# The output projection of a gated convolution, with its block product done as seven products of halves

## The chip, the cores and the metric

One NeuronCore of one Trainium2 chip runs the whole kernel. The metric is the device time of one execution in microseconds (us); smaller is better. The engines are named as the profile names them: PE (TensorE: matmuls, with PEld for its weight loads), DVE (VectorE), ACT (ScalarE), POOL (GpSimd) and SP (SyncE, which here only issues DMA transfers).

## The reference

One layer of a diffusion trunk on 1024 tokens of width 1024, float32. `ada_terms` makes six rows from a conditioning vector. The change is in the line `(gate_b * conv) @ w_out` and the two after it:

```python
def short_conv_mixer(h, w_in, conv_w, w_out, on_grid):
    gate_b, gate_c, hv = jnp.split(h @ w_in, 3, axis=-1)
    u = gate_c * hv
    conv = conv3_grid(u, conv_w) if on_grid else conv3_seq(u, conv_w)
    return (gate_b * conv) @ w_out

def swiglu(h, w_in, w_out):
    gate, up = jnp.split(h @ w_in, 2, axis=-1)
    return (jax.nn.silu(gate) * up) @ w_out

# in reference(), the one layer there is:
sh1, sc1, g1, sh2, sc2, g2 = ada_terms(cond_lat, ada_w[i], ada_b[i])
hl = modulate(rmsnorm(x, norm1_g[i]), sh1, sc1)
yl = short_conv_mixer(hl, conv_w_in[j], conv_w[j], conv_w_out[j], True)
x = x + g1 * yl
x = x + g2 * swiglu(modulate(rmsnorm(x, norm2_g[i]), sh2, sc2), ffn_w_in[i], ffn_w_out[i])
return rmsnorm(x, final_g)
```

## The kernel before, in words

**Numbers.** Every float32 operand of a matmul is kept as two tiles, a high half (a cast on ACT) and a low half (raw minus high, on DVE; `split`, lines 82 to 84). A product of two operands is three matmuls: high by high, high by low, low by high (`TERMS`). A matmul here is 128 by 128 times 128 by 512.

**Seven products.** The projections `h @ w_in`, `h @ ffn_w_in` and the last one, `@ ffn_w_out`, cut both matrices into two by two quarters and form the block product with seven products of (sums of) quarters instead of eight; they are named P1 to P7. P1, P6, P7 and P4 add up in one PSUM bank (X), P2 goes to Y, P5 and P3 go to Z. The convolution's output projection `@ w_out` alone is the plain product.

**Stages on PE, in the order of time.** First the adaLN columns and the first projection products (lines 421, 472). Then the mixes (line 522): 60 steps of 12 matmuls, six pairs of output tiles by five products. Then the output projection (line 1108): `y_steps` for eight tiles of 128 tokens. For a tile, eight pieces of 128 channels by two halves of the columns by three terms are 48 matmuls, with the token tile stationary and 512 columns of `w_out` moving. After a tile, `residual` (lines 1114 to 1139) multiplies by the row g1, adds x, takes the mean square and the scaled rows `xr`; `h2_of` (lines 1075 to 1090) transposes them on PE and applies the second shift and scale while PE leaves PSUM. Then the FFN: `Gate` objects (line 1183 on), each with seven products (line 632), the first three of them interleaved (`two`, `three`), the others in `in_turn`. Last the products of `ffn_w_out` (line 1537).

**What sets the order.** Up to the end of the mixes the order on SP, DVE, ACT and PE is written out by hand (`in_order`): at step t, first the loads of `ahead[t][0]` go to SP, then the sums and splits of the step, then the units of `ahead[t][1]`, then the 12 matmuls and what reads their result. POOL is left to the planner. From the output projection on, before the change, the planner of the tile framework orders all engines by priority, with a few `issue_after`.

**Tiles.** SBUF tiles come from pools with a fixed number of slots: `t_s` 32 slots of 4 KB a partition, `t_wop` 8 (halves of operands), `t_wraw` 5 (raw weights), `t4` 3, `t2` 6. A tile that finds no free slot makes its first writer wait. PSUM has 8 banks.

**Side work.** `AdaRow` objects `rows[0]` to `rows[5]` build the rows g1 (0, 1) and shift and scale for the second norm (2 to 5, into the DRAM row `rows3`): loads, scaling on ACT, an accumulating DMA on POOL, sums on DVE, a split, two matmuls over the partitions (line 291), an ACT copy (line 297) and a POOL store (line 299). `columns2` (lines 1141 to 1148) reads `rows3` back, transposes it on PE and makes `shift2` and `scale2`, which `h2_of` needs. The mixed channels, v, go to the DRAM tensor `vd` and come back as token tiles (`v_tile`).

## Time and profile before

| | us |
|---|---|
| Time, median of 3 runs (lowest, highest) | 989.28 (988.66, 989.86) |
| Span of the profiled execution, first to last instruction | 987.3 |
| PE busy in it | 978.7 |
| DVE, ACT, POOL busy in it | 721.0, 488.7, 121.3 |
| Mixes, by the chain of waits | 92.1 to 257.2 |
| Output projection | 257.2 to 351.4 |
| First three gates of the FFN | 351.4 to 412 |

The page gives no time for the profiled execution but its span; the runs' median stands 2.0 us above it (989.28 - 987.3). A matmul is shown with its own duration, about 0.39 us, but matmuls overlap: PE's rate is read from the chain of waits, where a row gives the time that so many matmuls in a row took. "PE busy" near 100% says only that PE is never without a matmul.

### The profile page before, as it was taken

To read this page: it belongs to the slowest core of one execution; us is meant where nothing else is said; L and a number is where in the kernel's file an instruction comes from. 1 tells how busy PE (TensorE), PEld (TensorE's weight loads), DVE (VectorE), ACT (ScalarE), POOL (GpSimd) and SP (SyncE) were. 2 spreads that over 40 slices of the span, in tenths; PEclk is the share of its full clock that TensorE was granted. 3 is DMA by queue.
4 is the path that set the end of the run, shared out by engine and by line. 5 is a ranking of instruction groups with operands and counts; after the bars stand their busy time and mean duration, and the time that the engine had idled before them with its cause. 6 is when DMAs were issued, how large, how long until landed. Compare 5 with 4: busy or idle time off the path is not lost.

```text
span 987.3 us, 12316 instructions
## 1 busy us (share of the span) xinstructions
PE 978.7 (99%) x4416; PEld 807.3 (82%) x4416; DVE 721.0 (73%) x1014; ACT 488.7 (49%) x784; POOL 121.3 (12%) x201
## 2 busy tenths in 40 slices
PE   9999999999999999999999999999999999999997
PEld 6788888887888888888888888888888888888886
DVE  6968988888656799765865765665665755878898
ACT  6766776656445675333333333333334353534464
POOL 2031001121111100320130110110110110000300
PEclk9999999999999999999999999999999999999999
DMA  9999399997874232633642331431315954577534
GB/s 298 318 340 321 99 274 280 296 283 222 251 229 149 86 120 86 179 118 96 197 123 75 128 118 58 146 117 54 128 65 202 388 189 155 175 260 278 186 107 170
DMA packets 156733, 181.77 MB, mean 184 GB/s; under 512 B 8406, under 2 KB 113086, under 8 KB 156672
## 3 DMA queue, kind: packets, MB, share of 16 engines
q1 hardware_dynamic: 143088, 138.50, 44.0%
q0 software_dynamic: 12784, 40.17, 13.1%
q10 hardware_dynamic: 800, 2.32, 0.6%
q8 instruction: 34, 0.56, 0.2%
q14 instruction: 27, 0.22, 0.1%
HBM read 135.33 MB, written 38.03 MB: 176 GB/s over the span
## 4 chain that ended last, share of the span: by engine, by line
PE 97%; DVE 1%; DMA 1%; ACT 0%; issue 0%; SPq 0%; POOL 0%; DVEq 0%; ACTq 0%
PE X_f L632 24%; PE zP L1537 21%; PE m L522 17%; PE Z_f L632 12%; PE y L1108 9%; PE Y_f L632 6%; PE x L421 3%; PE x L472 3%; DVE ada_acc L180 1%; PE x1T L1081 1%; DMA x<-in_x_dram 1%; PE xT L348 1%; PE ada_ps L192 1%; PE zl L1537 0%; PE ada_ps L291 0%
## 5 line engine op out<-in xcount | busy, mean ns | idle before, releaser
L74 DVE TENSOR_TENSOR BP_f<-wr_f,BP_f 128x512 fp32r<-128x512 f32 x154 | 105.0, 687 | 63.4 <-ACT BP_f L83 61.3
L83 ACT CAST BP_f<-wr_f 128x512 fp32r<-128x512 f32 x154 | 94.8, 621 | 88.1 <-PE Z_f L632 62.8
L1537 PE MATMUL zP<-w3h_P,a3l_P 128*128 128x512 f32 (+1 forms) x308 | 118.6, 385 | 0.0
L1537 PE MATMUL zP<-w3l_P,a3h_P 128*128 128x512 f32 (+1 forms) x308 | 118.6, 385 | 0.0
L1537 PE MATMUL zP<-w3h_P,a3h_P 128*128 128x512 f32 (+1 forms) x308 | 117.2, 385 | 0.0
L1537 PEld LDWEIGHTS zP<-w3h_P,a3h_P 128*128 128x128 f32 x308 | 57.9, 188 | 11.7
L1537 PEld LDWEIGHTS zP<-w3l_P,a3h_P 128*128 128x128 f32 x308 | 57.9, 188 | 11.7
L1537 PEld LDWEIGHTS zP<-w3h_P,a3l_P 128*128 128x128 f32 x308 | 57.9, 188 | 11.4
L74 DVE TENSOR_TENSOR a3l_P<-a3l_P,a3h_P 128x1024 fp32r<-128x1024 f32 (+1 forms) x42 | 47.2, 1129 | 21.7 <-ACT a3h_P L1337 21.7
L632 PE MATMUL X_f<-AS3h,BP_f 128*128 128x512 f32 x176 | 57.7, 389 | 0.0
L632 PE MATMUL X_f<-A22h,BP_f 128*128 128x512 f32 x176 | 57.6, 389 | 0.0
L632 PE MATMUL Z_f<-AS4h,BP_f 128*128 128x512 f32 x176 | 57.6, 389 | 0.0
L632 PE MATMUL X_f<-AS2h,BP_f 128*128 128x512 f32 x176 | 57.6, 389 | 0.0
L632 PE MATMUL Y_f<-A12h,BP_f 128*128 128x512 f32 x176 | 57.5, 390 | 0.0
L632 PE MATMUL X_f<-A11h,BP_f 128*128 128x512 f32 x176 | 57.4, 389 | 0.0
L632 PE MATMUL Z_f<-AS1h,BP_f 128*128 128x512 f32 x176 | 57.4, 389 | 0.0
L1108 PE MATMUL y<-woh,vh_t 128*128 128x512 f32 x128 | 50.4, 394 | 0.0
L1108 PE MATMUL y<-woh,vl_t 128*128 128x512 f32 x128 | 49.9, 390 | 0.0
L1108 PE MATMUL y<-wol,vh_t 128*128 128x512 f32 x128 | 49.8, 389 | 0.0
L74 DVE TENSOR_TENSOR wr_f<-wr_f,wr_f 128x512 f32<-128x512 f32 x66 | 45.3, 688 | 1.6
L1337 ACT CAST a3h_P<-a3l_P 128x1024 fp32r<-128x1024 f32 (+1 forms) x42 | 40.7, 977 | 10.4 <-DMA a3l_P<-ad_S 6.9
L77 DVE TENSOR_TENSOR u_f<-Z_f,u_f 128x512 f32<-128x512 f32 x22 | 15.2, 690 | 37.9 <-ACT u_f L649 35.4
(349 smaller groups left out, 2371.4 us busy)
## 6 DMA issues: line engine op xcount, KB each, us to landing
wr_f<-in_ffn_w_in_dram SPq DMA_DIRECT2D x44, 512.0 KB, 3.7
ada_w<-in_ada_w_dram SPq DMA_DIRECT2D x60, 256.0 KB, 5.8
w_P<-in_ffn_w_out_dram SPq DMA_DIRECT2D x30, 512.0 KB, 5.7
a3l_P<-ad_S SPq DMA_DIRECT2D x20, 512.0 KB, 6.8
ad<-a POOLq DMA_DIRECT2D x33, 256.0 KB, 2.6
ada_w<-in_ada_w_dram SPq DMA_DIRECT2D x16, 512.0 KB, 5.4
a3l_P<-ad SPq DMA_DIRECT2D x15, 512.0 KB, 3.7
wr<-in_conv_w_in_dram SPq DMA_DIRECT2D x12, 512.0 KB, 8.0
```

The source lines that it names most:

```text
L74: return nc.vector.tensor_tensor(o, a, b, op=ALU.subtract)
L77: return nc.vector.tensor_tensor(o, a, b, op=ALU.add)
L83: nc.scalar.copy(hi, raw)
L180: nc.vector.scalar_tensor_tensor(acc, self.rows[r], by, acc, op0=ALU.mult, op1=ALU.add)
L192: nc.tensor.matmul(self.ps[j][:, j:j + 1], lhsT=part[:, j, :], rhs=by, start=j == 0 and r == (*self.direct, "sum")[0], stop=j == 1 and r = ...
L421: nc.tensor.matmul(xbank[pair], lhsT=w0[k][wi][:, place[pair], :], rhs=h_of(k, 0)[hi], start=(k == 0 and i == 0), stop=(k == KD - 1 and i ...
L472: nc.tensor.matmul(xbank[self.pair], lhsT=self.w[wi][:, k, :], rhs=h_of(half * KH + k, 0)[hi], start=(half == 0 and k == 0 and i == 0), st ...
L522: nc.tensor.matmul(self.ps[a], lhsT=self.w[pname][wi][:, k, a * P:(a + 1) * P], rhs=A[aname, k // 2][hi][:, k % 2, :], start=(q == 0 and k ...
L632: mm = nc.tensor.matmul(ps, lhsT=w[:, wi, 2 * kp + kk, :], rhs=A[aname, kp][hi][:, kk, :], start=(first and kp == 0 and kk == 0 and i == 0 ...
L1108: mm = nc.tensor.matmul(ys[t][n], lhsT=vt[t][vi][:, k, :], rhs=wo[k][wi][:, n * H:(n + 1) * H], start=(k == 0 and i == 0), stop=(k == KD - ...
L1337: nc.scalar.copy(hi, f(lo))
L1537: mm = nc.tensor.matmul((zs[t] if to is None else to)[:, cols], lhsT=a[ai][:, k % 2, t * P:(t + 1) * P], rhs=w[wi][:, k % 2, cols], start= ...
```

## The change

The output projection becomes seven products of halves too. The token tile j (of the first 512 tokens) and the tile j + 4 (of the last 512) are a pair; channels and columns are cut into halves. For each of seven products there are four steps, one for each pair, of 12 matmuls (two `kp`, two `n`, three terms), in the fixed order P1, P2, P5, P6, P7, P4, P3; they are the steps 60 to 87, and the first 17 steps of the FFN's first three gates follow as steps 88 to 104, in the same written order. Step 60 is called `Y0`, step 88 `F0`.

- g1 is multiplied into the quarters of `w_out` (`w_scale`, on DVE) instead of into the result. Sums of quarters of `w_out` are formed in place on DVE (`ws`, `w2`, `w4`, `n`), one sum of the token operand on DVE (`vs`), the others by accumulating DMAs on POOL (`v+`).
- Signs are put into the mixes (`mul_negated`) and into P6's weights.
- Half of v stays in SBUF; `vd` has four channel tiles, not eight.
- x is added by accumulating DMAs on POOL for the left half of the first tokens' columns and for all of the last tokens'; for the right half of the first tokens' it is loaded on SP into the tile to which P4's result is added. The scaling by 1/rms goes from ACT to DVE (`x`), `h2_of` becomes `h2_pair` (two tiles at once, in the middle of a product's matmuls, `mid`).
- The sums of `rows[4]` and `rows[5]` move from steps 49 to 58 to the steps 70 to 74, their matmuls to the steps 79 and 77; `load_rows3` goes from POOL to SP at step 80; `columns2` is at step 83.
- The load of g1 goes to step 50. The loads of the first three gates go to the steps 69, 72 and 74, their sums and splits one by one (`gs`, `gh`, `gl`) to the steps 74 to 100.
- In `in_turn`, loads of ada rows for g2 start one gate later (`waited`).

```diff
-    vd = dram.tile([KD, P, T], F32, name="vd")
+    vd = dram.tile([KH, P, T], F32, name="vd")
+    def mul_negated(o, a, b):
+        nc.vector.scalar_tensor_tensor(o, a, -1.0, b, op0=ALU.mult, op1=ALU.mult)
...
-                ((33, 34, 35, 36), (37, 38, 39, 40), (49, 50, 51, 53)),
-                ((42, 43, 44, 45), (46, 47, 48, 49), (55, 57, 57, 58)))
+                ((33, 34, 35, 36), (37, 38, 39, 40), (70, 71, 72, 73)),
+                ((42, 43, 44, 45), (46, 47, 48, 49), (71, 72, 73, 74)))
...
-                also(at_sum[3] + 2, lambda r=r: rows[r].row(rows3))
+                also(at_sum[3] + (6 if r == 4 else 2), lambda r=r: rows[r].row(rows3))
...
-        def output_split(k):
-            raw, = wo[k]
-            wo[k] = [t_sr(f"wo{s}_{k}", [P, D]) for s in "hl"]
-            split(*wo[k], raw)
...
+        def w_scale(name, kp):
+            d0 = (int(name[0]) - 1) * H
+            mul(wr[name, kp], wr[name, kp], g1[:, None, d0:d0 + H].broadcast_to([P, 2, H]))
...
+        def w_high(pname, name, kp):
+            wop[pname, kp] = [t_sr(f"wo{s}_{pname}_{kp}", [P, 2, H]) for s in "hl"]
...
+        def v_add(o, x, kp):
+            ps = [v_parts(name, kp) for name in (o, x)]
+            for n in range(2) if any(len(p) > 1 for p in ps) else (slice(0, 2),):
+                nc.gpsimd.dma_start(*[p[0][1][:, n, :] if len(p) == 1 else p[n][1] for p in ps], accum_op=ALU.add)
+        YPLAN = {"P1": "X", "P2": "Y", "P5": "Z", "P6": "X", "P7": "X", "P4": "X", "P3": "Z"}
...
+        def y_product(pname, j, between):
...
+            for kp in range(2):
+                for n in range(2):
+                    if 6 * kp + 3 * n in between:
+                        between[6 * kp + 3 * n]()
+                    for i, (vi, wi) in enumerate(TERMS):
+                        nc.tensor.matmul(ybank[into, j], lhsT=vop[pname, kp][vi][:, n, j * P:(j + 1) * P],
+                                         rhs=wop[pname, kp][wi][:, n, :],
...
+        def y_after(pname, j):
+            ps = ybank[YPLAN[pname], j]
+            a, b = j, j + TH
+            if pname == "P1":
+                x1a[j] = t_s(f"x1_{a}", [P, D])
+                nc.scalar.copy(x1a[j][:, L], ps)
+                nc.gpsimd.dma_start(x1a[j][:, L], x[a * P:(a + 1) * P, L], accum_op=ALU.add)
+                nc.sync.dma_start(x1a[j][:, R], x[a * P:(a + 1) * P, R])
+            elif pname == "P2":
+                sub(x1a[j][:, L], x1a[j][:, L], ps)
+                square(a, x1a[j], L)
+                mean_half(a, L)
+            elif pname == "P5":
+                x1b[j] = t_s(f"x1_{b}", [P, D])
+                nc.scalar.copy(x1b[j][:, R], ps)
+            elif pname == "P6":
+                add(x1b[j][:, L], ps, x1b[j][:, R])
+            elif pname == "P7":
+                add(x1b[j][:, R], ps, x1b[j][:, R])
+                nc.gpsimd.dma_start(x1b[j], x[b * P:(b + 1) * P, :], accum_op=ALU.add)
+            elif pname == "P4":
+                add(x1a[j][:, R], ps, x1a[j][:, R])
+                square(a, x1a[j], R)
+                normed(a, x1a[j], R, L)
+            else:
+                add(x1b[j][:, L], ps, x1b[j][:, L])
+                square(b, x1b[j], L)
+                normed(b, x1b[j], L, R)
...
+        also(50, load_g1)
...
+        at_step(Y0, ("c", "12", 1), ("wl", "P2", "12", 0), ("wh", "P2", "12", 1), ("vh", "P2", "21", 0), ("wl", "P2", "12", 1), ("vh", "P2", "21", 1))
+        at_step(Y0 + 1, ("c", "21", 0), ("vl", "P2", "21", 0), ("c", "22", 0))
+        at_step(Y0 + 2, ("vl", "P2", "21", 1), ("vs", 0), ("vs", 1))
+        at_step(Y0 + 3, ("c", "21", 1), ("ws", 0), ("wh", "P5", "21", 0))
+        at_step(Y0 + 4, ("vh", "P5", "11", 0), ("vh", "P5", "11", 1), ("c", "22", 1), ("vl", "P5", "11", 0), ("v+", "11", "22", 0))
+        at_step(Y0 + 5, ("vl", "P5", "11", 1), ("v+", "11", "22", 1), ("ws", 1), ("wh", "P5", "21", 1), ("wl", "P5", "21", 0))
+        at_step(Y0 + 6, ("wl", "P5", "21", 1), ("w2", 0), ("wh", "P6", "21", 0))
...
+        at_step(Y0 + 16, ("vh", "P4", "21", 0), ("wl", "P3", "12", 0), ("gh", 1, "P1", t_sr), ("vl", "P4", "21", 0))
+        at_step(Y0 + 17, ("vh", "P4", "21", 1), ("wl", "P3", "12", 1), ("gl", 1, "P1"), ("vl", "P4", "21", 1), ("gh", 0, "P2", t_sr))
...
+        loads(Y0 + 20, load_rows3)
+        also(Y0 + 23, columns2)
...
+        mid = {Y0 + 24: (6, "m", 0), Y0 + 25: (9, "m", 2), F0: (3, "m", 4), F0 + 2: (9, "m", 6)}
...
-    def y_steps(t, ks, at=None, then=None):
-        if t not in ys:
-            ys[t] = [bank(f"y{t}_{n}") for n in range(2)]
-        for k in ks:
-            for n in range(2):
-                for i, (vi, wi) in enumerate(TERMS):
...
-        elif pieces:
+        elif pieces and waited:
             start_piece(p, t_wraw)
+        waited.append(p)
```

More of the change, by code (lines that the diff above doesn't have):

```diff
@@ L623, in products @@
+        def products(self, *names, between=()):
             for name in names:
@@ new lines, in trunk_kernel, with load_rows3, columns2 @@
+    rows3s = []
+    def load_rows3():
+        rows3s.append(t2("rows3s")[:2 * KD, :P])
+        nc.sync.dma_start(rows3s[0], rows3.rearrange("o j (k p) -> (o j k) p", p=P))
+    def columns2():
+        rows, = rows3s
+        ps = bank("cols3")
+        nc.tensor.transpose(ps[:, :2 * KD], rows, ident[:2 * KD, :2 * KD])
+        add(shift2, ps[:, :KD], ab[:, 3 * KD:4 * KD])
+        add(scale2, ps[:, KD:2 * KD], ab1[:, 4 * KD:5 * KD])
+        mul(scale2, scale2, g2c)
+    order = [ft for i in range(FH) for ft in (i, i + FH)]
@@ new lines, in trunk_kernel, with __init__, weights, c11 @@
+    class Gate(Pair):
+        def __init__(self, ft, where=t_wraw):
+            self.ft = ft
+            super().__init__(f"f{ft}", [ffn_w_in[:, j * FF + ft * P:j * FF + (ft + 1) * P] for j in range(2)], where)
+        def weights(self):
+            super().weights()
+            if self.ft == order[-1]:
+                start_output()
+        def c11(self, ps, p1):
+            self.sa = t2(f"sa_{self.ft}")
+            add(self.sa, ps, p1)
+            nc.scalar.activation(self.sa, self.sa, AF.Silu)
+        def c21(self, ps):
+            self.sc = t2(f"sc_{self.ft}")
+            nc.scalar.activation(self.sc, ps, AF.Silu)
+        def c22(self, ps, u3):
+            add(u3, ps, u3)
+        def c12(self, ps, u2):
+            add(u2, ps, u2)
+        def finish(self):
+            at = self.at = t_s(f"a_{self.ft}", [P, 2, H])
+            mul(at[:, 1, :], self.u3, self.sc)
+            mul(at[:, 0, :], self.u2, self.sa)
@@ new lines, in trunk_kernel, with h_sum @@
+        gates = []
+        for n, t in ((0, 9), (1, 12), (2, 14)):
+            loads(Y0 + t, lambda n=n: gates.append(Gate(order[n], t_s if n == 2 else t_wraw)))
+        s2 = [None] * 2
+        def h_sum(name, kp):
+            r11, r12, r21, r22 = h2[0][kp], h2[0][kp + 2], h2[1][kp], h2[1][kp + 2]
+            if name == "S1":
+                s2[kp] = t_s(f"S1_{kp}f", [P, 2, H])
+                add(s2[kp], r21, r22)
+            elif name == "S2":
+                sub(s2[kp], s2[kp], r11)
+            elif name == "S3":
+                sub(r21, r11, r21)
+            else:
+                sub(r12, r12, s2[kp])
@@ L1349, in start_output @@
                 low3(*operand3)
-    in_turn(itertools.chain(three[2:], map(Gate, order[3:])), NF - 2, between_gates)
+    in_turn(itertools.chain(three[2:], map(later_gate, order[3:])), NF - 2, between_gates)
     top, bot = [None] * TH, [None] * TH
```

477 lines of the change are left out of this document (262 added, 215 removed).

## The prediction

> **What bounds the kernel now.** I read the page first (busy times, chain of waits), then what PE waits for, then the chain in order of time around the output projection, then busy times by stage.
>
> ```profile
> span 987.3 us, 12316 instructions
> ...
> PE 978.7 (99%) x4416; PEld 807.3 (82%) x4416; DVE 721.0 (73%) x1014; ACT 488.7 (49%) x784; POOL 121.3 (12%) x201
> ...
> PE 97%; DVE 1%; DMA 1%; ACT 0%; issue 0%; SPq 0%; POOL 0%; DVEq 0%; ACTq 0%
> ```
> ```profile
> PE idle_ps L125 <- DVE rows L102: 1.7, 1, 1.7
> PE x L421 <- ACT A11h L376: 0.3, 1, 0.3
> PE xT L348 <- DVE x L342: 0.3, 1, 0.3
> ```
>
> PE is 97% of the chain, and the list of its waits is three entries long, 2.3 us in all, and none is of a line of the stages here (125 is the warm-up, 421 and 348 the first projection). So where the change is, PE never waits: a matmul less is its own time less, and a wait more is its own length more.
>
> ```profile
> 257.18 5.44 PE y L1108 x24
> 262.62 0.47 PE ada_ps L291 x2
> ...
> 288.96 0.16 PE cols L1145
> ...
> 325.06 10.92 PE y L1108 x48
> 335.98 0.87 PE x1T L1081 x8
> 336.85 10.90 PE y L1108 x48
> ...
> 351.38 4.76 PE X_f L632 x21
> ```
>
> The chain in order of time (start, length, what): 48 matmuls in a row take 10.92 us, 0.2275 each; I use that rate and not the 0.39 us of one matmul, since they overlap. The projection runs from 257.18 to 351.38. A step of 12 matmuls is 2.73 us.
>
> ```profile
> 92.00:257.20 165.20, 165.20 (x728) 135.60 (x727) 143.76 (x160) 109.35 (x152) 21.10 (x29) 1.00 0.85 244
> 257.20:351.40 94.20, 94.20 (x444) 78.11 (x444) 61.82 (x101) 49.52 (x79) 14.56 (x26) 1.00 0.55 175
> 228.00:257.20 29.20, 29.20 (x129) 23.47 (x128) 26.47 (x34) 16.75 (x25) 3.14 (x5) 1.00 0.74 235
> 351.40:375.00 23.60, 23.60 (x109) 19.61 (x109) 23.18 (x34) 18.28 (x33) 1.16 (x2) 1.00 0.31 97
> ```
>
> Busy times by stretch (length, then PE, PEld, DVE, ACT, POOL, then PE's granted clock, DMA share, GB/s). In the projection DVE has a third of the time free (61.82 of 94.20), ACT half. The last two rows are the densest DVE stretches beside a full PE: 26.47 of 29.20 and 23.18 of 23.60. DVE can be almost full without a PE wait.
>
> **The change, part by part.**
>
> *Matmuls.* Before: 8 token tiles x 8 channel pieces x 2 halves x 3 terms = 384. After: 7 products x 4 pairs x 12 = 336. The 48 that go are one row of the chain: **-10.9 us**. Shapes stay (128x128 weights, 512 columns), so I keep the rate. The transposes stay 64, the matmuls over ada rows move but stay as many. All of the gain is here; the rest of the change can only take some of it back.
>
> *DVE.* The steps 60 to 87 put the preparation of seven products where plain splits stood. DVE's prices:
>
> ```profile
> L74 DVE TENSOR_TENSOR wr<-wr,wr 128x1024 f32<-128x1024 f32 x24 | 29.2, 1215 | 0.0
> L74 DVE TENSOR_TENSOR wr_f<-wr_f,wr_f 128x512 f32<-128x512 f32 x66 | 45.3, 688 | 1.6
> L585 DVE SCALAR_TENSOR_TENSOR cv<-u,cols,cv 128x1008 f32<-128x1008 f32 x16 | 20.0, 1261 | 0.3 <-ACT cv L581 0.2
> ```
> ```profile
> 258.93 4.62 DVE L74 TENSOR_TENSOR wol<-wor,woh 128x1024 fp32r<-128x1024 f32 x4
> 346.08 3.70 DVE L74 TENSOR_TENSOR BP_f<-wr_f,BP_f 128x512 fp32r<-128x512 f32 x6 [0.95 <-ACT BP_f L83]
> ```
>
> Back to back they overlap a little: from the second fence a 1024-wide one comes every (4.62 - 1.22)/3 = 1.13 us, a 512-wide one every (3.70 - 0.69)/5 = 0.60. The scalar_tensor_tensor forms (the negated products, P6's low halves) are 4 to 9% dearer by the L585 row; that is half a microsecond in all.
>
> Counted in the steps 60 to 77. Of 1024 elements: 5 scalings by g1, 10 sums of weights and tokens (`vs`, `ws`, `w2`, `w4`, `n`, two each), 12 low halves of weights (P2, P5, P6, P7, P4, P3), 6 of tokens (P5, P6, P7): 33 x 1.13 = 37.3. Of 512 elements: 8 low halves of tokens that lie in two tiles (P2, P4), 8 for the moved ada rows, 2 for gate weights, 10 reads of PSUM (P2 four, P6 four, P7 two): 28 x 0.60 = 16.8. With the half microsecond, **54.6 us of DVE in 18 steps of PE, which are 18 x 2.73 = 49.1**, plus 0.5 for the moved matmuls of `rows[5]` at step 77. So DVE falls behind by about 5 us here. Does PE notice? Counting from PE's start of step 60, DVE begins about 0.7 later (its last operation of step 59 reads PSUM) and has P4's last token half, the operation before the last of step 77, at 0.7 + 54.6 - 0.6 = 54.7. PE wants it in the second half of step 80: 20 x 2.73 + 0.5 + 1.4 = 56.5. That leaves **1.8 us of room**, if DVE is never idle in 54. The earlier deadlines have the same or more room (P5's second half: DVE 21.4 against PE 23.2; P6 and P7 more). At the idle share of the stretch 351.4:375 (0.42 of 23.60) DVE would idle 1 us: no wait. At that of 228:257.2 (2.73 of 29.20) 5.1 us: PE waits 3.3. Bounds 0 to 3.3; I take **0.5**, nearer to the denser row, because that stretch too is one of splits and sums in a fixed mix with PSUM reads. After step 77 DVE has 3 operations of 512 a step and catches up. Over steps 84 to 101 I count 52 us of DVE against 18 x 2.73 + 7.0 (64 transposes, 8 for 0.87) = 56: it fits.
>
> *ACT.* High halves, PSUM copies and squares of the same 18 steps add to about 38 of 49 us (casts 1.05 and 0.62, copies 0.59):
>
> ```profile
> L83 ACT CAST woh<-wor 128x1024 fp32r<-128x1024 f32 x8 | 8.1, 1048 | 3.5 <-DMA wor<-in_conv_w_out_dram 3.5
> L297 ACT COPY ada_b<-ada_ps 1x512 f32<-1x512 f32 x2 | 1.1, 574 | 0.8 <-PE ada_ps L291 0.8
> ```
>
> Taken at nothing: its work lies beside DVE's, which is longer. At step 75 the `t_s` tiles I count are 34 for 32 slots; P3's high halves then wait for P6's to be freed, at PE's end of step 75, where DVE is still behind. P3 wants them at step 84: no cost; without that cover at most a step of ACT, again before step 84.
>
> *The rows for the second norm.* `rows[4]`'s matmuls move to step 79, and `columns2`, a PE instruction in strict order at step 83, needs what they make: ACT copy, POOL store to DRAM, then a load, now on SP.
>
> ```profile
> 266.13 0.52 POOL L299 DMA_DIRECT2D rows<-ada_b  x1 [5.16 <-ACT ada_b L297]
> 271.72 0.52 POOL L1143 DMA_DIRECT2D rows3s<-rows  x1 [5.07 <-DMA rows<-ada_b]
> ```
> ```profile
> rows3s<-rows POOLq DMA_DIRECT2D x1, 8.0 KB, 4.7
> ada_w<-ada_w POOLq DMA_DIRECT2D x12, 512.0 KB, 6.9
> g<-g_row POOLq DMA_DIRECT2D x1, 512.0 KB, 8.4
> ```
>
> From the POOL issue to the landed load: 271.72 - 266.13 + 4.7 = 10.3. With the two matmuls (0.5), the ACT copy (0.6) and the hand-overs that is about 11.7, against 4 x 2.73 = 10.9 between the steps 79 and 83. It comes **0.8 late**; behind the instruction wait step 83's matmuls and all of PE. Before, the same chain had PE's work from 263.1 to 288.9 for cover. If PE waits at step 80 for DVE, that wait covers this one. What could make it worse is POOL's order: the accumulating DMA that adds x after P7's third pair waits for a DVE sum that is some 5 us behind. Ahead of the store it would hold it by that. Bounds 0 to 5.5; I take **0.8**, since the store is ready first when DVE is behind, and POOL's order is the planner's.
>
> *g1.* Its load (8.4 us to landing) goes from behind the mixes to step 50, and DVE, in order, waits for it with the splits of the mixes behind it. The slot in `t_wraw` is free by step 43 or so, and the row is in DRAM since step 38. I take nothing: steps 50 to 59 need some 24 us of DVE by the same prices (10 operations of 1024 elements, 4 of 1008, 13 smaller) against 27.3, and the mixes' halves are made five steps ahead. If POOL issues it only at step 50, DVE loses up to 8.4, gains 3.3 back by step 60, brings 5.1 into the stretch with 1.8 of room and PE loses 3.3.
>
> *Accumulating DMAs.* Twelve of `v+`, eight for x. The first `v+` for P6 can go when P5's token low is made (15 us into the stage); two on POOL and a landing of 6.9 (the `ada_w` row) end by 26; ACT's cast for P6 follows, P6 starts at 32.8: hidden with 5 to spare. Those for P7 and P4 have more.
>
> *The Trainium skill, "SBUF — State Buffer", § SBUF: two separate sides*, speaks against this: GpSimd, which makes the descriptors of POOL's DMAs, shares a port pair with VectorE and is locked out for the whole of some VectorE instructions. In the trace an accumulating issue on POOL lasts 0.83 to 0.97 beside a DVE that is 87% busy. Each POOL issue delayed by one DVE operation more, an estimate of 1.2 us, would make the sum 1.2 worse, through the chain of the rows alone.
>
> *The rest.* SP gets six gate loads of 512 KB at the steps 69 to 74 and `load_rows3` behind them; their slots come free at the steps 64 to 73, so SP is not stuck at step 80. Fewer bytes move (four reads and four stores of v fewer, DMA share 0.55 before). From step 88 on PE's work is that of before, in another hand-written order; from the fourth gate on the order is as before but for the ada loads one gate later, needed only at line 1537's products. I take nothing.
>
> **Sum:** 987.3 - 10.9 + 0.5 + 0.8 = 977.7 of span; with the 2.0 by which the runs' median stands above this span, **979.7 us**.
>
> **The rivals.**
>
> 1. *DVE or POOL comes late by some microseconds.* The upper ends: 3.3 (DVE idles as in 228:257.2) or 5.5 (the store behind x's accumulate), or g1 late on DVE, 3.3; they cover one another in part, since each wait lets DVE catch up. Together 4 to 7: 982.5 to 985.5, say **984**. For it: DVE's load above PE's in 18 steps. Against: the room, and two dense stretches without a PE wait. The Trainium skill, "TensorE: Matmul & The Clock Gate", § Part 1: The HAM clock gate, says an idle window of about 3.4 us halves PE's clock until it has been busy as long; by that an estimate of 1.7 more. The granted clock is 1.00 in every row above, and no PE wait of that length lies between work here to test it.
>
> 2. *Slower: DVE in strict order stalls at every low half.* A low half follows its high half on ACT, which follows a sum on DVE. In the mixes that has a price:
>
> ```profile
> L74 DVE TENSOR_TENSOR BP6l_m<-wr,BP6h_m 128x1024 fp32r<-128x1024 f32 x6 | 7.3, 1222 | 6.7 <-ACT BP6h_m L83 6.7
> L74 DVE TENSOR_TENSOR BP4l_m<-wr,BP4h_m 128x1024 fp32r<-128x1024 f32 x6 | 7.3, 1222 | 5.4 <-ACT BP4h_m L83 5.4
> L74 DVE TENSOR_TENSOR BP3l_m<-wr,BP3h_m 128x1024 fp32r<-128x1024 f32 x6 | 7.3, 1216 | 0.0
> ```
>
> 0 to 1.1 us of idle for one (6.7/6). The stretch has 26 groups of low halves. It decides from (1.8 + 10.9)/26 = 0.49 us each: then the gain is gone. At the mean of the two upper rows, 1.0, DVE loses 26, PE 24, less what the waits give back; at 0.6, 13.8, and the time is **992**. Against: in the mixes DVE waits because it has nothing else; here sums and other splits are written between a high and its low half.
>
> 3. *No wait at all:* 989.28 - 10.9 = **978.4**. It is the lower end of my forecast rather than another case.
>
> **How the numbers follow.** Forecast (978.4 to 981.9, waits of 0 to 3.5): 0.64. Rival 1 (982 to 986.5): 0.24. Rival 2 (from 987 up): 0.09. Below 978.4, by something in the later stages that I don't see: 0.03. The range leaves out rival 2 and the top of rival 1: 977.8 to 985.5. A change of 0.2% (2 us) is about what a measurement of this kernel can tell from none. Faster by more is below 987.3: 0.91; within it 0.04; slower 0.05, both from rival 2.
>
> **What would show it.** Matmuls of the projection 336, their 48 still 10.9 us. PE's waits: at most two new ones, at P4's first pair for a DVE low half, and at the transpose of `columns2` for the load of `rows3s`. The first x1T transposes about 70 us after the projection starts. DVE over 90% busy for the first 50 us of the projection. I am wrong if PE waits at P2 to P7 for DVE or ACT again and again (rival 2), if the first wait is at P1 (g1), or if the stage ends with no wait and the time has not fallen by 10.

## The result, and the profile after

After the change the kernel takes 982.26 us (981.23 to 982.75, 4 runs) against 989.27 (988.66 to 989.86): a ratio of 0.9926, 95% interval 0.9912 to 0.994. It is 7.0 us faster, inside the forecast's range of 977.8 to 985.5 and 2.6 us behind the forecast of 979.7.

The page of the changed kernel, then the list of what PE waits for (us in total, times, longest):

```profile
span 980.6 us, 12243 instructions
...
PE 970.0 (99%) x4368; PEld 798.9 (81%) x4368; DVE 746.9 (76%) x1027; ACT 494.4 (50%) x811; POOL 135.1 (14%) x209
...
PE 86%; DVE 8%; DMA 2%; issue 1%; ACT 1%; SPq 0%; POOL 0%; DVEq 0%; ACTq 0%; POOLq 0%
```
```profile
PE Z_f L656 <- DVE AS4l L74: 0.7, 1, 0.7
...
PE x1T L761 <- DVE xr L1261: 0.6, 2, 0.4
PE yX L1238 <- DVE x L77: 0.2, 1, 0.2
PE yX L1238 <- DVE vl_P L74: 0.2, 1, 0.2
```

PE has exactly 48 matmuls fewer (4368 for 4416). But DVE, 1% of the chain before, is now 8% of it, and four entries of the wait list are new: 0.2 and 0.2 at the projection's products (line 1238), 0.6 at the transposes (761), 0.7 at the first gate (656).

Where the span went is read from the chain of waits at two places where both kernels do the same work: the first product of the mixes (`m`) and the last product of all (`zl`). The chain of the changed kernel, then that of the kernel before (start, length, what):

```profile
92.90 2.27 PE m L529 x10
...
970.43 3.97 PE zl L1730 x33
```
```profile
92.09 2.95 PE m L522 x13
...
977.39 3.97 PE zl L1537 x33
```

Between them lie 881.50 us after (970.43 + 3.97 - 92.90) and 889.27 before: 7.77 less, where 48 x 0.2275 = 10.92 were taken out. So PE lost **3.15 us** to waits. The starts of its matmuls show where. A wait of the list costs more than its row says: in the row of `AS4l` below, 0.74 us is the listed wait, but the matmul before it starts at 384.91, so 1.13 lies between the two starts instead of 0.23, and the next start again is 0.34 away instead of 0.23. That is 1.0 us for a listed 0.74.

```profile
384.91 0.39 PE L656 MATMUL Z_f<-AS4h,BP_f 128*128 128x512 f32 x1
386.04 0.50 PE L656 MATMUL Z_f<-AS4l,BP_f 128*128 128x512 f32 x1 [0.74 <-DVE AS4l L74]
386.38 0.62 PE L656 MATMUL Z_f<-AS4h,BP_f 128*128 128x512 f32 x2
```

By starts alone the losses are 0.14 at P5 (at 280.3 us), 0.37 and 0.32 at P7 (301.3, 303.5), 0.34 and 0.59 at two groups of transposes (326.8, 341.3) and 0.90 here: 2.66, and 0.1 more for the start after each. A second profile of the same kernel has the same stretch (881.47) without the 0.34 at 326.8, so a loss of that size comes and goes. The other 1.1 us of the span lie outside the stretch: the mixes start 0.81 later, and what follows the last product is 0.26 longer (980.6 - 974.40 against 987.3 - 981.36). The experiments below give this stretch too, each from one profile, since the part ahead of it varies by up to 1 us between profiles.

Why P7 waits is in DVE's timeline of the changed kernel (start, us):

```profile
299.30 1.22 DVE L74 TENSOR_TENSOR vl_P<-v,vh_P 128x1024 fp32r<-128x1024 f32 x1
300.43 0.69 DVE L77 TENSOR_TENSOR x<-yX,x 128x512 f32<-128x512 f32 x1
301.03 0.69 DVE L74 TENSOR_TENSOR ada_l<-ada_w,ada_h 128x512 fp32r<-128x512 f32 x1
301.63 0.69 DVE L77 TENSOR_TENSOR ada_w<-ada_w 128x512 f32<-128x512 f32 x1
302.23 1.22 DVE L74 TENSOR_TENSOR vl_P<-v,vh_P 128x1024 fp32r<-128x1024 f32 x1
```

DVE runs without a break. The PSUM bank that PE needs at 301.0 is read at 300.43 to 301.12; the low half of the second token half is ready at 303.45, and two operations of a moved ada row stand ahead of it. DVE is fully used and some tenths late. Its idle time in the stretch of the predicted 18 steps (groups of lines of DVE from 257.2 to 306.3; the last column is idle time before the group) stands at two low halves only:

```profile
L74 DVE TENSOR_TENSOR wol_P<-wo,woh_P 128x1024 fp32r<-128x1024 f32 x7 | 8.6, 1222 | 0.0
L74 DVE TENSOR_TENSOR vl_P<-v,vh_P 128x1024 fp32r<-128x1024 f32 x6 | 7.3, 1222 | 2.3 <-ACT vh_P L1211 2.3
```

### The profile page after: what moved, and what is told of

Its sections match the earlier page's. It is cut to its first block, busy times and chain, and to the rows that moved or that the text cites. A ratio compares the mean times of both kernels' runs of the same rounds, so it can differ in the third digit from the quotient of the medians.

```text
span 980.6 us, 12243 instructions
## 1 busy us (share of the span) xinstructions
PE 970.0 (99%) x4368; PEld 798.9 (81%) x4368; DVE 746.9 (76%) x1027; ACT 494.4 (50%) x811; POOL 135.1 (14%) x209
## 4 chain that ended last, share of the span: by engine, by line
PE 86%; DVE 8%; DMA 2%; issue 1%; ACT 1%; SPq 0%; POOL 0%; DVEq 0%; ACTq 0%; POOLq 0%
PE X_f L656 24%; PE zP L1730 21%; PE m L529 16%; PE Z_f L656 12%; PE Y_f L656 6%; PE x L472 3%; PE x L421 2%; DMA ada_w<-in_ada_w_dram 2%; DVE vl_P L74 1%; DVE wol_P L74 1%; DVE ada_acc L180 1%; PE x1T L761 1%; DVE x L77 1%; DVE wo L77 1%; DVE wo L80 1%
## 5 line engine op out<-in xcount | busy, mean ns | idle before, releaser
L1730 PEld LDWEIGHTS zP<-w3h_P,a3h_P 128*128 128x128 f32 x308 | 57.8, 188 | 11.7
L1730 PEld LDWEIGHTS zP<-w3l_P,a3h_P 128*128 128x128 f32 x308 | 57.9, 188 | 11.5
L656 PE MATMUL Y_f<-A12h,BP_f 128*128 128x512 f32 x176 | 57.4, 389 | 0.0
L656 PE MATMUL Z_f<-AS1h,BP_f 128*128 128x512 f32 x176 | 57.4, 389 | 0.0
L656 PEld LDWEIGHTS X_f<-AS3h,BP_f 128*128 128x128 f32 x176 | 33.0, 188 | 7.0 <-ACT e_f L670 0.2
L656 PEld LDWEIGHTS Y_f<-A12h,BP_f 128*128 128x128 f32 x176 | 33.0, 188 | 6.9
L656 PEld LDWEIGHTS Z_f<-AS1h,BP_f 128*128 128x128 f32 x176 | 33.0, 188 | 6.8
```

Of the source, the lines that this page charges most:

```text
L656: mm = nc.tensor.matmul(ps, lhsT=w[:, wi, 2 * kp + kk, :], rhs=A[aname, kp][hi][:, kk, :], start=(first and kp == 0 and kk == 0 and i == 0 ...
L1730: mm = nc.tensor.matmul((zs[t] if to is None else to)[:, cols], lhsT=a[ai][:, k % 2, t * P:(t + 1) * P], rhs=w[wi][:, k % 2, cols], start= ...
```

## The experiments

**The 48 matmuls alone, in the old order.** The kernel before without one of its eight channel pieces (that eighth of the projection's sum is left out):

```diff
@@ y_steps, the kernel before
+            if k == 3:
+                continue
```

> The kernel before with one of the eight channel pieces of the output projection left out (k = 3: 16 groups of three matmuls, 48 in all); that piece's part of the product is missing, all else is done. Theory: PE alone sets the end there, a matmul costs 0.2275 us, so this is what the 48 matmuls are worth without the rest of the change: -10.9 us, 978.4. Rival: PE at that rate would find a wait behind it (DVE, ACT or a load of a token tile is hardly hidden); then less than 9 us is gained, and part of what the change failed to gain is no price of its other edits.

Measured: 985.81 us (984.83 to 987.94, 6 runs), ratio 0.9968 (0.9956 to 0.998). It falls by 3.4, not by 10.9. PE's waits in it:

```profile
PE x1T L1081 <- ACT xr L1140: 2.4, 3, 1.2
...
PE Z_f L632 <- DVE AS1l L74: 1.7, 1, 1.7
PE y L1110 <- ACT vh_t L83: 1.2, 1, 1.2
```

New waits of 5.3 us, 6.5 by the starts: the span of the profiled execution, the fastest of the six, fell by 987.3 - 983.0 = 4.3, which is 10.9 less 6.6. So in the kernel before, PE's list of waits was short because PE was just long enough; 48 matmuls less uncovered the scaled rows for the transposes, the high halves of the tokens and the low half of the first gate. The changed kernel keeps about 7 of the 10.9 where the old order keeps 3 to 4. Not all of that need be the written order: the changed kernel also adds x by DMAs, scales by 1/rms on DVE and takes the token tiles in pairs, and which of these keeps how much was not separated.

**The same without the norm's chain.** In addition the squares and roots are left out, and `xr` is an unscaled copy for the first seven token tiles:

```diff
@@ residual, the kernel before without 48 matmuls
-            nc.scalar.activation(xt, x1, AF.Square, accum_out=ss[0])
-            r = rstd_of(ss[0], f"x1_{t}")
+            pass
...
-            nc.scalar.mul(xt, x1, r)
+            nc.scalar.copy(xt, x1)
```

> The kernel before without one of the eight channel pieces (48 matmuls, as in the earlier run) and without the squares and the reciprocal roots of the norm: xr is an unscaled copy of the residual for the first seven token tiles, so norm and output differ. Theory (with 48 matmuls less the way residual, squares, root, scaling, transposes of one token tile is longer than PE's work beside it): PE's waits at the x1 transposes, 2.8 us by the starts, go, and the time is about 983, 2.8 below the earlier 985.8; the waits at the projection's matmuls and the first gate stay. Rival (the transposes wait because ScalarE or VectorE is late with other work, the splits): the waits stay and the time is within 1 us of 985.8.

Measured: 982.76 us (980.11 to 983.88, 6 runs), ratio 0.9928 (0.9916 to 0.9939), 3.05 below the kernel above. PE's waits, second view its stretches by granted clock (length, busy PE, PEld, DVE, ACT, POOL, then the clock):

```profile
PE y L1110 <- ACT vh_t L83: 1.7, 1, 1.7
PE X_f L632 <- ACT e_f L646: 0.4, 1, 0.4
...
PE Z_f L632 <- DVE AS1l L74: 0.2, 1, 0.2
```
```profile
273.00:274.00 1.00, 1.00 (x5) 0.78 (x4) 0.77 (x2) 0.27 (x1) 0.00 (x0) 0.68 1.11 294
274.00:275.00 1.00, 1.00 (x4) 0.81 (x3) 0.00 (x0) 0.63 (x1) 0.00 (x0) 0.50 1.12 299
...
276.00:277.00 1.00, 1.00 (x4) 0.82 (x3) 0.68 (x1) 0.00 (x0) 0.00 (x0) 0.61 1.02 279
```

All waits at the transposes are gone, as the theory said, so the way from the residual over squares, root and scaling to the transposes was the second bound. The edit also takes the squares off ACT, but the rival (ACT late with the splits) is out by the trace of the kernel above. There ACT has nothing to do for 3.16 us ahead of the scaling that PE waits longest for; it waits for the root from POOL, and likewise for 0.65 and 0.96 us ahead of the scaling for the other two waits:

```profile
340.04 1.15 ACT L1140 ACTIVATE xr<-x,x_r 128x1024 f32<-128x1024 f32 x1 [3.16 <-POOL x_r L313]
```

The other two waits were to stay. The one for the tokens' high halves did and grew from 1.2 to 1.7 us; the first gate's fell from 1.7 to 0.2, with 0.4 new beside it, so it hung on the norm's chain too. From the mixes to the last product this profile is 1.7 us shorter than the one above (883.45 against 885.17); 1.6 us in it go to the lower clock, told at the end.

**How much room VectorE has.** The changed kernel with the low halves of the weights of P2 and P5 computed twice (same values), 4 x 1.13 = 4.5 us more of DVE:

```diff
@@ w_low
-                sub(lo, wr[name, kp], f(hi))
+                for _ in range(2 if pname in ("P2", "P5") else 1):
+                    sub(lo, wr[name, kp], f(hi))
```

> The changed kernel with the low halves of P2's and P5's weights computed twice (the same values written again): four DVE operations of 1024 elements more, 4.5 us, in the steps 60 to 66. Theory: the room of DVE against PE is used up by step 73, so nearly every microsecond more becomes a wait of PE at P6 or P7: 4 us or a little more, about 986.5. Rival (there is still room, the waits at P7 have another cause): under 1 us, 983.

Measured: 987.78 us (986.29 to 988.27, 10 runs), ratio 0.9982 (0.9973 to 0.9991). From the mixes to the last product it takes 886.37, which is 4.9 more than the changed kernel. Its waits, and the two stretches up to P5's second wait (at 284.62) and after it:

```profile
PE yZ L1239 <- DVE wol_P L74: 4.5, 2, 3.1
```
```profile
257.20:284.70 27.50, 23.04 (x101) 18.43 (x100) 25.95 (x27) 11.88 (x20) 12.15 (x14) 1.00 0.86 168
284.70:340.00 55.30, 54.77 (x254) 44.19 (x255) 51.59 (x74) 38.41 (x78) 12.96 (x19) 1.00 0.67 165
```

The added 4.5 us come back as 4.5 us of waiting, all of it at P5 and none at P6 or P7, where the theory had put it. At P5 the room was zero, not 1.8; the 55 us behind it show no wait that the changed kernel hadn't.

**Without the sums.** The changed kernel without the ten sums of weights and tokens on DVE; the seven products then combine the wrong quarters:

```diff
@@ UNITS
-        UNITS = {"w4": last_sum, "w2": next_sum, "vs": first_sum, "ws": second_sum, ...
-                 "n": third, ...
+        UNITS = {**dict.fromkeys(("w4", "w2", "vs", "ws"), lambda kp: None), ...
+                 "n": lambda kp: None, ...
```

> The changed kernel without the ten in-place sums on DVE (first_sum, second_sum, next_sum, last_sum, third), which leaves the quarters' sums out of the products; PE's work, the casts, the low halves and the DMAs stay. Theory (DVE is a few us behind in steps 60 to 77, and the waits of 0.4 and 0.3 us at P7 are the price): 11 us less of DVE work takes both waits away, 0.7 us, and leaves the waits of 0.3 to 0.9 us behind the transposes and at the first gates: about 981.5 against the changed kernel's 982.3. Rival (DVE's sums delay also what follows, the scaled rows and the FFN's operands): all waits go, 2.5 us or more, 979.5.

Measured: 980.19 us (980.03 to 980.41, 4 runs), ratio 0.9907 (0.9894 to 0.9921): 2.1 below the changed kernel. Its list of waits:

```profile
PE Z_f L656 <- DVE AS4l L74: 0.7, 1, 0.7
PE x1T L761 <- DVE xr L1261: 0.4, 1, 0.4
```

The time lies between the theory's 981.5 and the rival's 979.5. Every wait at the products is gone; two behind them stay, with some 11 us of DVE less (ten sums of 1.13). So those two are not made by DVE's amount of work in the steps 60 to 77. From the mixes to the last product it takes 880.04, 1.46 less than the changed kernel; the waits at P5, at P7 and at 326.8 were 1.17 by the starts, and 0.1 more for the start after each. The rest of the 2.1 lies ahead of the mixes.

**The rows for the second norm one step later.** The matmuls of `rows[4]` at step 80 instead of 79, its load at 81 instead of 80:

```diff
-                also(at_sum[3] + (6 if r == 4 else 2), lambda r=r: rows[r].row(rows3))
+                also(at_sum[3] + (7 if r == 4 else 2), lambda r=r: rows[r].row(rows3))
...
-        loads(Y0 + 20, load_rows3)
+        loads(Y0 + 21, load_rows3)
```

> The changed kernel with the matmuls and the store of the ada row of rows[4] one step later (80 instead of 79) and its load on SP at step 81. Theory: from those matmuls to the landed load the changed kernel's trace has 10.4 us, of which about 11.5 lie between the steps 79 and 83; with one step less PE waits some 2 us at the transpose of columns2: 984. Rival: the planner lets POOL issue the store before x's accumulating DMA now and the chain takes 9 us or less: under 1 us.

Measured: 981.66 us (981.61 to 982.09, 4 runs), ratio 0.9923 (0.9909 to 0.9937), and no wait at the transpose of `columns2`. From the mixes to the last product it takes 881.47 us, as the changed kernel does. POOL's timeline in it, then POOL's and SP's in the changed kernel. The last line of each is from the view of the tensor `rows`: the shortest, middle and longest time from issue to landing of its three transfers between 300 and 330 us, which are the store of `rows[5]` (1.6 in both), the store of `rows[4]` and the load.

```profile
311.13 0.86 POOL L1288 DMA_DIRECT2D x<-in_x_dram  x1 [2.72 <-DVE x L77]
313.92 0.54 POOL L299 DMA_DIRECT2D rows<-ada_b  x1 [1.92 <-ACT ada_b L297]
DMA to landing us min/median/max: 1.6/2.9/3.2
```
```profile
311.96 0.86 POOL L1288 DMA_DIRECT2D x<-in_x_dram  x1 [2.74 <-DVE x L77]
312.53 0.82 POOL L299 DMA_DIRECT2D rows<-ada_b  x1
317.69 0.34 SPq L776 DMA_DIRECT2D rows3s<-rows  x1
DMA to landing us min/median/max: 1.6/3.4/5.0
```

In the changed kernel the row's matmuls start at 310.46, the store is issued 2.1 later and lands after 5.0, the load on SP follows at once and lands after 3.4, at 321.1, and PE comes to the transpose at 321.93: **0.8 us of room**. In the delayed kernel the matmuls start at 312.38, the store is issued 1.5 later and lands after 2.9, the load lands after 3.2, at 320.1, and PE comes at 321.13: 1.0 us. So the step of delay (2.73 us) is not swallowed by room. The chain from the matmuls to the landed load became shorter, 7.8 us in place of 10.6, as the rival said (9 or less).

What differs is where the store falls. In the changed kernel POOL issues it 0.6 us behind an accumulating DMA of x (512 KB), in the delayed one 2.8 behind. The other profiles agree: 0.5 to 0.8 us behind such a DMA the store landed in 4.8 to 5.4, and 2.1 behind it in 3.5.

**Four variants beside each other.** First the changed kernel once more.

> The changed kernel as it is, once more, beside the three variants of it. Theory: 982.3 again, with a clean clock at the start of the profiled execution the span is nearer 980 than 980.6. Rival (the lower clock at the start of the profiled execution belongs to the change): the clock falls below 0.95 in the first 30 us again.

Measured: 982.54 us (981.74 to 983.05, 5 runs), ratio 0.993 (0.9916 to 0.9943). Its span is 980.6 again and its granted clock is 1.00 at the start, so the low clock there (last section) isn't the change's. That the span would be nearer 980 did not come: the mixes start at 92.88, as late as in the first profile. In the profiles of all these kernels, whose code is the same up to there, they start between 91.9 and 92.9; the 0.8 us are no step of the change.

Second, the six sums of the moved ada rows on GpSimd:

```diff
+        for r in (4, 5):
+            rows[r].adder = lambda o, x, y: nc.gpsimd.tensor_tensor(o, x, y, op=ALU.add)
```

> The six sums of the moved ada rows (row groups 4 and 5) on GpSimd instead of VectorE, all else as after the change. Theory (P7's second half came late because these sums, 3.6 us, stand ahead of its low half on VectorE): the waits of 0.37 and 0.32 us at P7 go, 0.7 us less than the changed kernel, about 981.6, and P5's 0.14 may go too. Rival (the sums are not it, or GpSimd's slower sums hold up the accumulating DMAs and the rows' way to the second norm instead): same time or 1 to 3 us more, with a new wait at the transpose of columns2 or of P4.

Measured: 982.6 us (982.16 to 983.13, 5 runs), ratio 0.9933 (0.9921 to 0.9946): no gain, and from the mixes to the last product 882.08, 0.6 more than the changed kernel. The waits at P7 and P5 went, as the theory said, and others came, in the mixes: 1.0 (for `p`, at 243.9) and 0.3 us in the list of PE's waits. The rival had the place wrong but the time right. POOL's and DVE's timeline in this kernel, then DVE's at the same operations after the change:

```profile
238.48 3.70 POOL L1100 TENSOR_TENSOR ada_w<-ada_w,ada_w 128x512 f32<-128x512 f32 x2 [7.93 <-DMA ada_w<-ada_w]
242.25 2.15 POOL L1100 TENSOR_TENSOR ada_w<-ada_w 128x512 f32<-128x512 f32 x1
```
```profile
239.31 1.72 DVE L74 TENSOR_TENSOR BP3l_m<-wr,BP3h_m 128x1024 fp32r<-128x1024 f32 x1
240.95 2.31 DVE L80 TENSOR_TENSOR wo<-wo,g 128x1024 f32<-128x1024 f32 x1
```
```profile
240.16 1.22 DVE L74 TENSOR_TENSOR BP3l_m<-wr,BP3h_m 128x1024 fp32r<-128x1024 f32 x1
241.29 1.22 DVE L80 TENSOR_TENSOR wo<-wo,g 128x1024 f32<-128x1024 f32 x1
```

A sum on POOL takes 1.5 to 2.3 us (of the two in the first row the second starts at 239.91 and takes 2.27) where DVE needs 0.69, and beside it DVE's own operations go from 1.22 to 1.72 and 2.31: the work moved away came back as a slower DVE, at a place where DVE had no more than some tenths of room: the `p` that PE then waits for is DVE's next operation. The Trainium skill, "SBUF — State Buffer", § SBUF: two separate sides, states a lock between an operation of GpSimd that reads SBUF and one of VectorE with two inputs in SBUF. The trace agrees. The two engines take turns: the first sum ends at 239.95, DVE's low half at 241.03, the second sum at 242.18, DVE's scaling at 243.26, each about 1.1 us after the other engine's. And a `p<-m,z` at 238.71, which reads `m` from PSUM, keeps its 0.68 us beside the first sum.

Third, three places of the written order, with nothing added or removed:

```diff
-        at_step(Y0 + 20, ("vh", "P3", "22", 0), ("vl", "P3", "22", 0))
-        at_step(Y0 + 21, ("vh", "P3", "22", 1), ("vl", "P3", "22", 1))
+        at_step(Y0 + 20, ("vh", "P3", "22", 0), ("vl", "P3", "22", 0), ("vh", "P3", "22", 1))
+        at_step(Y0 + 21, ("vl", "P3", "22", 1))
...
-        at_step(Y0 + 26, ("gl", 0, "P5"), ("gs", 1, "P5"), ("gh", 1, "P5", t_sr))
-        at_step(Y0 + 26, ("hh", "11", 0), ("hh", "11", 1), ("hl", "11", 0))
+        at_step(Y0 + 26, ("hh", "11", 0), ("gl", 0, "P5"), ("gs", 1, "P5"), ("hh", "11", 1), ("gh", 1, "P5", t_sr), ("hl", "11", 0))
...
-        at_step(F0 + 13, ("hs", "S4", 0), ("hh", "S4", 0), ("hs", "S4", 1), ...
+        ("hs", "S4", 0) at the end of F0 + 11, ("hs", "S4", 1) at the end of F0 + 12
```

> After the change with three places of its written order altered and no operation added or taken away: the sums S4 of the gate's halves one and two steps earlier, the cast of A11 first in step 26 of the projection's second part, the second high half of P3 one step earlier. Theory (the waits at the end of the projection are made by ScalarE's and VectorE's order, not by the amount of work): the gaps of 0.90 (first gate, AS4), 0.59 and 0.34 us (transposes of x1) go, 1.8 us less than the changed kernel, about 980.5. Rival (these waits come from VectorE still being behind from the earlier steps): they only move, and the time stays within 0.4 us of the changed kernel.

Measured: 980.95 us (980.49 to 981.87, 4 runs), ratio 0.9917 (0.9904 to 0.9931), and in a second series, beside the next kernel but one, 980.79 (980.39 to 981.57, 4 runs), ratio 0.9914 (0.99 to 0.9927):

> The three altered places of the written order once more, as the kernel to compare with on the same chip. Theory: 980.9 again, with a first gate that waits 0.8 us for ScalarE's copy of a PSUM bank in place of the 0.9 for VectorE's low half of AS4. Rival (part of the first run's gain was the undisturbed clock): above 981.5.

The waits at the transposes and at `AS4l` are gone; which of the three places took which was not separated. A new one stands in the first gate, after the planner moved the order of its products:

```profile
PE X_f L656 <- ACT e_f L670: 0.7, 1, 0.7
```

From the mixes to the last product it is 1.1 us shorter than the changed kernel beside it (880.40 against 881.47), and in the second series 880.38. The rest of the difference between the two spans (978.7 against 980.6) is the earlier part, where the edit does nothing.

Fourth, both edits together.

> Both edits of the two kernels before this one together. Theory: the gaps add, 0.7 + 1.8 = 2.5 us less than the changed kernel, about 979.7, and the starts of PE's matmuls after 80 us lie only about 1.6 us in all above the steady rate. Rival (one cause behind both): no more than the larger of the two alone, 980.5 or above.

Measured: 981.37 us (981.31 to 983.04, 5 runs), ratio 0.9924 (0.9911 to 0.9936). The gains don't add: with GpSimd's sums the 1.1 and 0.3 us in the mixes come along. It is 0.4 above the order alone by the medians and 0.9 from the mixes to the last product (881.32).

**P7's low half ahead of the moved row.** The altered order, and the row's split and scaling (301.03 and 301.63 in the timeline of after) behind the token's low half:

```diff
-        at_step(Y0 + 13, ("vh", "P7", "12", 1), ("wh", "P4", "22", 0), ("vl", "P7", "12", 1))
+        ("vh", "P7", "12", 1) at the end of Y0 + 12
+        ahead[Y0 + 13][0].append(lambda: UNITS["vl"]("P7", "12", 1))
+        at_step(Y0 + 13, ("wh", "P4", "22", 0))
```

> The kernel with the three altered places of the written order, and in addition the low half of P7's second token half ahead of the moved ada row's split and scaling on VectorE (two operations of 512 elements, 1.2 us, change places with it). Theory (P7's second wait is made by this order alone, and GpSimd's sums only moved work into a fuller place): the wait of 0.34 us at P7's second weight goes and no other comes, 0.3 us less than the three altered places, about 980.6 against 980.9. The other 0.3 us at P7, for the copy of a PSUM bank, stay. Rival (VectorE is behind by more than these two operations, or the row's split is missed next): a wait of 0.3 us or more turns up at the next product P4 or at the row's matmuls, and the time is the same or longer.

Measured: 981.16 us (980.77 to 982.49, 5 runs), ratio 0.9918 (0.9905 to 0.9932). No gain; the rival held. The wait for `vl_P` is gone, and the next to come late is the row itself:

```profile
PE ada_ps L291 <- DVE ada_l L74: 0.3, 1, 0.3
```

From the mixes to the last product it takes 880.52, against 880.38. So at P7 DVE is behind in both orders that were tried. The altered order without this edit has the lowest median of the kernels that compute the layer: 980.8 to 980.9, about 8.4 us below the kernel before.

## Why the prediction was right or wrong

**The matmuls** (-10.9): right. 336 matmuls are left in the projection, and the stretch from the mixes on is shorter by 10.9 less the waits. **"All of the gain is here; the rest of the change can only take some of it back": wrong.** In the old order 48 matmuls less are worth 3.4, so the rest of the change gives as well as takes. The row that misled me was the short list of waits: "a matmul less is its own time less" does not hold there for 48, and the list can't show how far the next chain stands behind. I should have worked out that chain in the old order too.

**VectorE's term** (+0.5, bounds 0 to 3.3): the size about right, the place wrong. By the starts 0.14 at P5 and 0.69 at P7, about 1.1 with the starts behind. The prediction gave P4 the least room, 1.8, and "the same or more" to the earlier ones. Measured, P5 had none. DVE idled 2.3 us at the tokens' high halves (the row above), the 1.42 of it at 273.57 just ahead of P5: ACT's order there has the cast of P5's weight first, and that waits for a sum of DVE.

```profile
271.06 1.05 ACT L1182 CAST woh_P<-wo 128x1024 fp32r<-128x1024 f32 x1 [4.88 <-DVE wo L77]
272.01 0.58 ACT L1274 COPY x<-yX 128x512 f32<-128x512 f32 x1
272.49 2.00 ACT L1211 CAST vh_P<-v 128x1024 fp32r<-128x1024 f32 x2
```

From there to P5's weight DVE has no pause, so without the 1.42 that weight's low half, 0.14 late, would have had room. So "ACT at nothing" also falls in part: by its share of busy time it had room, by its order it made DVE idle. The idle 2.3 lies between the 1 and the 5.1 of the two rows I had chosen from, and the count of DVE's work was right: the last token half came at 57.4 in place of 54.7, later by about that idle time. P6's low halves, priced 4 to 9% dearer, took 1217 ns, as the others did. P4, wanted at 56.5 in my count, got its last token half at 314.6 by DVE's timeline, and PE came to it at about 315.0, by the count of steps, since P7 had made PE later: no wait, with 0.4 to spare.

**The rows for the second norm** (+0.8, bounds 0 to 5.5): 0 measured, by 0.8 us of room. The sum had 11.7 us needed against 10.9. Measured are 10.6 needed, since from the store's issue to the landed load it takes 8.6 (312.53 to 321.09) instead of 10.3, mostly by the load on SP (3.4, not 4.7), while the store came 2.1 after the matmuls' start and not 1.4. And there are 11.5 for it (310.46 to 321.93): the row's own two matmuls, 0.5, take PE's time as well, and I had put them on the chain's side alone. POOL's order did cost something here: behind x's DMA the store took 5.0 us, and where it stood clear of it 2.9 to 3.5. The term was close to its edge, and it came out at nothing by two errors of about 1 us and 0.5 us.

The Trainium skill's rule that I weighed beside it ("SBUF — State Buffer", § SBUF: two separate sides) would have made the sum 1.2 us worse. The page names the operations of VectorE that lock GpSimd's descriptors out, those in a mode with two ports, and says that a `tensor_tensor` has none; from 257.2 to 306.3 DVE runs only `tensor_tensor` and two `scalar_tensor_tensor`. The trace agrees: POOL's issues for x take 0.85 to 0.86 (rows above) beside a DVE that is busy almost without a break, as before the change. For DMA issues no run here shows the lock.

**"The rest" from step 88 on** (0): wrong, and the largest miss. The transposes and the first gate lose 0.34 + 0.59 + 0.90 = 1.8 by the starts, about 2.1 with the starts behind; the 0.34 is at step 84, ahead of the part so named, and is missing in the second profile. I had taken the order behind the stage as neutral because PE's work is the same; but in the planner's order PE had no wait there at all, and the hand-written one puts a sum of S4 too late for its high and low half, and the casts of A11 behind others. The altered order shows that the order makes these waits: they go without any work going, though 0.7 us come back at another product. The prediction's totals for DVE in the steps 84 to 101 (52 of 56) fit and said nothing of that.

**g1** (0): right. POOL issued its load at 213.92, after 8.7 us of waiting for a slot, and it landed 8.0 later; DVE scales by it from 241.29 on, without idle time. **The accumulating DMAs** (0): right; those of `v+` land in 7.6 to 7.7 (middle values) instead of the assumed 6.9, those of x in 4.8 and 5.8, and no wait of PE or DVE names them.

**Around the stage** (2.0, from the runs' median): 1.7 here (982.26 - 980.6), and the profiled span has 1.1 us that the sum didn't have, 0.8 of them in code that the change doesn't touch.

**The rivals.** Rival 1 (984) named the mechanism, lateness of DVE, but it cost 1.1, not 4 to 7. Rival 2 decides from 0.49 us a group and 26 groups; 2.3 us of idle make 0.09 each, at two of them. Rival 3 (no wait) fails on 3.15 us. My case, waits of 0 to 3.5, held with 3.15, though not at the places that I had named. Its time, 978.4 to 981.9, did not hold: 982.26, and 982.54 in the repeat, lie just above it and inside rival 1's 982 to 986.5, since 1.1 us of the span came from outside the stretch. That the measured time lies in the range of 977.8 to 985.5 is in part luck: of the 1.3 us of waits in the sum, DVE's 0.5 came as 1.1 and the rows' 0.8 did not come, and the largest loss stood in a term that I had put at nothing. Of the marks that I had set, DVE over 90% busy in the first 50 us came true (47.6 of 50), and so did the first transpose about 70 us after the start (326.3 - 257.2 = 69.1); "at most two new waits" of PE did not.

## What to carry to other kernels

When one engine is the bound almost alone, take the removed work out of its timeline and ask of each chain beside it when it would be late: here the old order returned 3.4 us of 10.9 when 48 matmuls were left out, and the changed kernel, with a new order and another way to the transposes, returned 7. In a written order check each deadline in turn against the engines' orders, not the stage's sums: the room at P5 was zero where the count had 1.8, and the waits that could be mended without less work (1.1 us) lay at the stage's end and behind it, where the order was new and PE's work was not. A chain of small transfers should be priced with what stands ahead of it in its queue: the same store took 2.9 or 5.0 us. Where an engine is full, moving single operations past a deadline, or onto GpSimd beside it, moved the wait and did not remove it here.

## What the runs showed of the hardware that was not expected

**The clock after a wait.** In the kernel without the norm's chain, PE waits 1.7 us for `vh_t` at 270 to 271.7, and the granted clock is 0.50 from 273.4 to 276.8, 3.4 us in all (the rows above); eight matmuls there start 0.427 us apart instead of 0.2275, which costs 1.6 us beside the wait. In the kernel with the doubled low halves a wait of 3.1 us is followed by a clock of 1.00 (both of its rows), though five of its ten runs show a mean clock of 0.994 to 0.995 where the profiled one has 0.999, and its median stands 5.2 to 5.5 above the changed kernel's for 4.5 of waits. In the first profile of the changed kernel the clock falls for as long at 15.4 us, in the early part of the span and with no listed wait of PE in the 7 us before, and in its second profile not:

```profile
15.00:16.00 1.00, 0.96 (x5) 0.59 (x3) 0.46 (x2) 1.00 (x3) 0.00 (x0) 0.54 1.24 298
16.00:17.00 1.00, 1.00 (x3) 0.81 (x4) 0.90 (x2) 1.00 (x5) 0.00 (x0) 0.50 1.09 334
...
18.00:19.00 1.00, 1.00 (x4) 0.78 (x4) 0.96 (x3) 0.39 (x1) 0.00 (x0) 0.75 1.22 290
```

The Trainium skill, "TensorE: Matmul & The Clock Gate", § Part 1: The HAM clock gate, states a halved clock after an idle window of about 3.4 us, and a window that runs freely. The length and the half agree with these rows; that an idle time of 3.4 us is needed does not, since a wait of 1.7 us was followed by it and one of 3.1 us was not. What decides was not tried, and that the wait made the clock fall is not shown. As an estimate from these rows, a wait of PE of 1.7 us or more can cost 0 to 1.6 us on top.

**The price of a wait in PE's list** is more than its row: 0.74 listed were 1.0 us by the starts of the matmuls around it.

**A small store behind an accumulating DMA** of 512 KB on POOL's queue landed later: 4.8 to 5.4 us when issued 0.5 to 0.8 us behind it, 2.9 to 3.5 when 2.1 to 2.8 behind.

**GpSimd's sums beside VectorE** lengthened VectorE's operations with two inputs in SBUF by 0.5 and 1.1 us, and were themselves 1.5 to 2.3 us long. Beside its DMA issues they kept their time: in the 18 steps, in which the issues of `v+` fall, the groups of 1024 elements have means of 1.217 to 1.222 us.
